# Two transformer blocks with a product-key expert layer on one core: gather rows of the first token tile brought forward, 76 instead of 64 expert columns spilled, their splits on VectorE

## The chip, the cores and the metric

The kernel runs on one core of one Trainium2 chip. The metric is the time of one execution on the device in microseconds (us). A comparison uses the median of several runs; the profile is of one execution.

The engines are named as in the profile: PE is TensorE (matmuls), DVE is VectorE, ACT is ScalarE, POOL is GpSimd, SP is the engine that issues most DMAs. Each takes its instructions in the order of the program.

## The reference

Two blocks, 512 tokens of width 1024, batch 1, all in float32. The first block mixes tokens by retention and by a sparse attention, then has a convolved feed-forward network (FFN). The second mixes by a gated linear recurrence and a short convolution; its last part is the expert layer that the change is about:

```python
q = (xb @ w_query).reshape(T, 8, 2, 128)                    # 8 heads, two halves
s = einsum('thpk,hpnk->thpn', q, sub_keys)                  # 128 scores per half
top_s, top_i = top_k(s, 16)
cand_s = top_s[:, :, 0, :, None] + top_s[:, :, 1, None, :]  # 16 x 16 pairs
best_s, best_pos = top_k(cand_s, 16); idx = ...             # of 128*128 = 16384 experts
gate = softmax(best_s)
act = gelu(einsum('td,thkd->thk', xb, expert_u[idx]))
out = einsum('thk,thkd->td', gate * act, expert_v[idx])
```

So each token has 8 x 16 = 128 experts, each with a row of `u` and a row of `v`. The result is scaled, added to `x`, and normalised.

## The kernel before

**Tiling.** The tokens lie in four tiles of 128. A float32 product on PE is made of three: each operand is split into a high and a low part of a rounded type (`split`, L195 to L202: the high part by ACT at L200, the low by DVE or POOL at L201), and `mm3` (L204 to L208) adds low x high, high x low and high x high. A pair of split buffers is taken from the pool `wsp` (8 pairs), what comes from DRAM lands in the pool `wraw` (3 buffers); `unit` (L189) does both for a piece of weights of 128 x 1024.

**The expert layer.** Tile 0 and tiles 1 to 3 are handled in two ways. For tile 0, each of the 128 experts of a token is fetched by an indirect DMA that POOL issues (`gather`, L1064): 128 rows of `u`, each followed by a dot product with the token on DVE (L1076), and 128 rows of `v`, each accumulated into `acc0` on DVE (L1078 or L1081). They use four buffers `grow`. For tiles 1 to 3, 384 tokens, all 16384 experts are computed densely: 128 columns of `u` with 128 experts each (`expert_in`, L1055), the activations times a dense gate matrix, and 128 columns of `v`.

**Stages.** `peer` (L1022) runs these stages one behind the other in the program:

1. `route`, first part: 16 query projections, each with its scores and `top16` on DVE.
2. `route`, second part: for each tile the top 16 of the 256 candidates and their indices and gates, nearly all on DVE (L1110 to L1154).
3. `gates_dense` (L1179): in 12 steps `c` of 32 tokens, each of eight groups `t4` of four tokens, two one-hot matrices `A` (`ga`) and `B` (`gb`) of 128 x 128 are built per token, and one matmul (L1215) makes the token's 128 x 128 gates. They go to DRAM (`gD`).
4. `experts_out` (L1225): for each of 128 columns `j`, activations times gates, split again, times the column of `v`.

Columns of `u` need only the tokens, so 64 of them (every even one) are computed early, between the steps of stages 1 to 3, and spilled to DRAM (`actD`); L1039 says after how many steps how many. In stage 4 they are read back; the odd ones are computed there. The gather begins with stage 4, and `GBY` spreads it over 120 columns.

**Who builds `A`.** `GP, GA = (2, 6), (0, 4)` at L35: groups 2 and 6 on POOL (L1198), 0 and 4 on ACT (L1202, L1203: |i - iota|, then relu(1 - that); the gate then goes into `B`, four narrow instructions at L1205), the others on DVE (L1209). `B` of the groups that are not ACT's is one wide compare on DVE (L1212).

**What sets the order.** The program is written in the order above, and a scheduler of the framework then orders the instructions of each engine: it runs its own model of time and, where an engine is free in it, takes the first instruction in the program that is ready. An instruction late in the program can so come early if all that it waits for is a buffer. Once built, the order is fixed, and engines wait for each other by semaphores.

## Time and profile before

| | |
|---|---|
| median of 3 runs | 2284.07 us (2283.7 to 2288.77) |
| profiled execution | 2284.71 us |
| its span | 2282.9 us |
| PE busy | 2202.7 us (96%) |
| DVE busy | 1655.5 us (73%) |
| ACT busy | 918.3 us (40%) |
| POOL busy | 793.9 us (35%) |
| moved by DMA | 469.53 MB, mean 206 GB/s |

The span runs from the first to the last instruction of the program. The shares are means over stages with different limits, so they say little about one stage: PE's 96% is of the whole span, and its busy time counts pipelined matmuls by modelled ends. The chain of waits on the page holds only the last instructions here, so the stages are read by windows, by lines, and by the order of single instructions. A line of the profile is that of the helper that records the instruction (L200, L201 and L206 to L208 are such), so the names of the tiles tell them apart.

### The profile page before, as it was taken

What the parts mean: (1) busy time and instruction counts of PE and PEld (TensorE: products, weight loads), DVE (VectorE), ACT (ScalarE), POOL (GpSimd) and SP (SyncE); (2) the same over time, 40 slices, a digit from 0 to 9 for tenths busy, and PEclk for the clock granted to TensorE, in tenths of its full rate; (3) what the DMA queues carried; (4) which work ended last, traced back from release to release, by engine and by line L of the source; (5) the groups of instructions that cost most, each with busy time, mean ns of one, the idle gap of its engine ahead of it and who ended that gap; (6) DMA issues with size and microseconds to landing.
All of it is one profiled execution on the core that took longest, in us unless ns stands there. A gap on an engine that the chain in (4) does not pass through costs nothing. (4 is left out here: it accounts for less than half of the span.)

```text
span 2282.9 us, 32142 instructions
## 1 busy us (share of the span) xinstructions
PE 2202.7 (96%) x11849; PEld 1956.0 (86%) x11849; DVE 1655.5 (73%) x3081; ACT 918.3 (40%) x1540; POOL 793.9 (35%) x603
## 2 busy tenths in 40 slices
PE   7998999999999999999998989989999999999998
PEld 6786888888889888889998989978888888888886
DVE  5347657788526478556589999678888787888878
ACT  4225444433325443343243467623333333333332
POOL 2223110000002233222366688634343434444445
PEclk9999999999999999999999999999999999999999
DMA  8323006766222221053345446799999999999996
GB/s 283 90 69 115 16 1 218 244 213 230 94 91 96 87 80 56 20 174 113 116 149 154 151 180 249 285 340 348 331 343 343 348 342 338 341 330 349 336 347 214
DMA packets 165645, 469.53 MB, mean 206 GB/s; under 512 B 18800, under 2 KB 62704, under 8 KB 165360
## 3 DMA queue, kind: packets, MB, share of 16 engines
q1 hardware_dynamic: 128624, 333.25, 42.4%
q0 software_dynamic: 36864, 134.23, 16.1%
q8 instruction: 93, 1.52, 0.3%
q14 instruction: 64, 0.52, 0.1%
HBM read 422.31 MB, written 39.85 MB: 202 GB/s over the span
## 5 line engine op out<-in xcount | busy, mean ns | idle before, releaser
L206 PE MATMUL b<-hh,wlo 128*128 128x384 f32 (+2 forms) x1872 | 658.0, 352 | 8.6 <-DVE wlo L201 3.1
L207 PE MATMUL b<-hl,whi 128*128 128x384 f32 (+2 forms) x1872 | 656.2, 351 | 3.4 <-DVE hl L288 3.3
L208 PE MATMUL b<-hh,whi 128*128 128x384 f32 (+2 forms) x1872 | 655.1, 351 | 0.0
L200 ACT ACTIVATE whi<-raw 128x1024 fp32r<-128x1024 f32 (+1 forms) x405 | 423.9, 1053 | 367.7 <-PE b L208 168.6
L201 DVE TENSOR_TENSOR wlo<-raw,whi 128x1024 fp32r<-128x1024 f32 x330 | 406.2, 1233 | 197.3 <-ACT whi L200 190.8
L206 PEld LDWEIGHTS b<-hh,wlo 128*128 128x128 f32 x1872 | 355.6, 190 | 37.1 <-issue 4.4
L207 PEld LDWEIGHTS b<-hl,whi 128*128 128x128 f32 x1872 | 356.1, 190 | 30.7 <-DVE hl L288 3.8
L201 POOL TENSOR_TENSOR wlo<-raw,whi 128x1024 fp32r<-128x1024 f32 x75 | 197.8, 2650 | 528.4 <-ACT whi L200 518.4
L208 PEld LDWEIGHTS b<-hh,whi 128*128 128x128 f32 x1872 | 356.5, 190 | 24.7
L206 PE MATMUL b<-whi,wl 128*128 128x512 f32 x768 | 299.6, 390 | 10.4 <-DVE wl L1261 10.4
L208 PE MATMUL b<-whi,wh 128*128 128x512 f32 x768 | 300.7, 392 | 0.0
L207 PE MATMUL b<-wlo,wh 128*128 128x512 f32 x768 | 300.6, 391 | 0.0
L1073 POOL DMA_INDIRECT grow<-in_p_ur_dram,eid x128 | 169.4, 1323 | 244.3 <-DVE gact L1076 163.7
L1073 POOL DMA_INDIRECT grow<-in_p_v_dram,eid x128 | 163.1, 1274 | 221.6 <-DVE acc L1078 137.9
L1061 ACT ACTIVATE act<-b 128x384 f32<-128x384 f32 x114 | 55.6, 490 | 345.4 <-PE b L208 300.0
L206 PE MATMUL b<-whi,hl 128*128 128x512 f32 (+1 forms) x464 | 178.9, 387 | 3.4 <-DVE hl L254 2.1
L206 PEld LDWEIGHTS b<-whi,wl 128*128 128x128 f32 x768 | 144.7, 188 | 39.4 <-DVE wl L1261 10.7
L208 PE MATMUL b<-whi,hh 128*128 128x512 f32 (+1 forms) x464 | 177.8, 384 | 0.0
L207 PE MATMUL b<-wlo,hh 128*128 128x512 f32 (+1 forms) x464 | 177.7, 383 | 0.0
L208 PEld LDWEIGHTS b<-whi,wh 128*128 128x128 f32 x768 | 144.5, 188 | 30.3
L207 PEld LDWEIGHTS b<-wlo,wh 128*128 128x128 f32 x768 | 144.7, 188 | 29.0
L1078 DVE SCALAR_TENSOR_TENSOR acc<-grow,gact,acc 128x1024 f32<-128x1024 f32 x127 | 163.1, 1284 | 3.2 <-DMA grow<-in_p_v_dram,eid 2.2
(296 smaller groups left out, 2979.1 us busy)
## 6 DMA issues: line engine op xcount, KB each, us to landing
raw<-in_p_u_dram SPq DMA_DIRECT2D x128, 512.0 KB, 4.4
raw<-in_p_v_dram SPq DMA_DIRECT2D x128, 512.0 KB, 6.5
raw<-in_w_adaT_dram SPq DMA_DIRECT2D x48, 512.0 KB, 4.1
gD<-gst SPq DMA_DIRECT2D x48, 512.0 KB, 4.4
gt<-gD SPq DMA_DIRECT2D x16, 1536.0 KB, 12.5
raw<-in_w_up_dram SPq DMA_DIRECT2D x44, 512.0 KB, 4.2
raw<-in_w_t_dram SPq DMA_DIRECT2D x32, 512.0 KB, 3.7
acts<-actD SPq DMA_DIRECT2D x64, 192.0 KB, 5.6
```

What stands on the lines that cost most here:

```text
L200: nc.scalar.activation(hi, raw, AF.Copy)
L201: (eng or nc.vector).tensor_tensor(lo, raw, hi.bitcast(F32), op=ALU.subtract)
L206: mm(out, al, bh, start=start, stop=False)
L207: mm(out, ah, bl, start=False, stop=False)
L208: mm(out, ah, bh, start=False, stop=stop)
L1061: self.nc.scalar.activation(act, ps, AF.Gelu)
L1073: nc.gpsimd.indirect_dma_start(out=g, out_offset=None, in_=rows[n], in_offset=bass.IndirectOffsetOnAxis(ap=self.eid[:, s:s + 1], axis=0))
L1078: nc.vector.scalar_tensor_tensor(self.acc0, g, act[:, s:s + 1], self.acc0, op0=ALU.mult, op1=ALU.add)
```

## The change

- `NSPILL` 64 becomes 76: 76 columns are spilled, spread over the 128, and 52 (`fresh`) are computed in stage 4. Spilled activations are 384 wide (`NIN`) as before.
- The pace (L1039 before) becomes five pieces of steps, columns, gather rows and the engine for the low part of the split: 1 step with 3 columns and 15 with 3 on POOL, then 8 with 10, 24 with 40 and 20 gather rows, 24 with 20 and 22 gather rows, the low part of all these on DVE. Before, all 64 were split on POOL. So 42 gather rows are written ahead of stage 4; their buffers `grow` now live in a pool opened ahead of stage 1.
- Gates: POOL builds `A` of three groups (1, 3, 6) instead of two. ACT puts the gate into `A` by four narrow instructions (relu(gate - gate x |i - iota|), with a fourth table of negated gates), and `B` is one wide compare on DVE in all eight groups. `ga` and `gb` have 4 buffers each instead of 6.
- Pools: `wsp` is closed and opened again ahead of the second mixer (8 pairs) and of the expert layer (6 pairs). In stage 4 two more raw buffers are used in turn with the three. Activations there lie in 8 buffers, and four instead of three columns are computed ahead.

```diff
-NSPILL = 64
+NSPILL = 76
+NIN = 384
-GP, GA = (2, 6), (0, 4)
+GP, GA = (1, 3, 6), (0, 4)
+NACT = 8
...
     def unit(self, src, eng=None):
-        raw = self.wraw.tile([128, 1024], F32, name="raw")[:, :src.shape[-1]]
+        self.turn = (self.turn + 1) % len(self.raws)
+        raw = self.raws[self.turn].tile([128, 1024], F32, name="raw")[:, :src.shape[-1]]
...
             if n == 2:
+                wsp.close()
                 late = ctx.enter_context(tc.tile_pool(name="late", bufs=1, reuse_waits="tile"))
                 self.h2 = late.tile([128, D], F32, name="h2")
+            if n > 1:
+                wsp.close()
+                wsp = ctx.enter_context(ExitStack())
+                self.wsp = wsp.enter_context(tc.tile_pool(name=f"wsp{n}", bufs=8 if n == 2 else 6, reuse_waits="tile"))
...
+            self.grows = c0.enter_context(tc.tile_pool(name="grows", bufs=GROWS, reuse_waits="tile"))
+            g0 = [self.gather(P)]
+            fresh = [j for j in range(128) if (j + 1) * (128 - NSPILL) // 128 > j * (128 - NSPILL) // 128]
...
-                pace = [(1, 3), (15, 10), (32, 37), (24, 14)]
+                pace = [(1, 3, 0, nc.gpsimd), (15, 3, 0, nc.gpsimd), (8, 10, 0, nc.vector), (24, 40, 20, nc.vector),
+                        (24, 20, 22, nc.vector)]
...
-                        for _ in range((i + 1) * us // steps - i * us // steps):
-                            act = self.expert_in(self.gpool or Q, psp, 2 * j, nc.gpsimd, "ga" if self.gpool else "act")
-                            nc.sync.dma_start(self.actD[j], act)
-                            j += 1
+                        for _ in range(part(cols)):
+                            act = (self.gpool or Q).tile([128, NIN], F32, name="act", bufs=4)
+                            j = todo.pop(0)
+                            self.expert_in(act, psp, j, eng)
+                            nc.sync.dma_start(self.actD[self.slot[j]], act)
+                        _advance(g0, part(r0))
...
-                    if t4 in GP:
-                        for i in range(4):
-                            nc.gpsimd.tensor_scalar(A[:, i], iota, ii[:, i:i + 1], gg[:, i:i + 1], op0=ALU.is_equal,
-                                                    op1=ALU.mult)
-                    elif t4 in GA:
+                    if t4 in GA:
+
                         for i in range(4):
                             nc.scalar.activation(A[:, i], iota, AF.Abs, bias=ii[:, i:i + 1], scale=-1.0)
-                        nc.scalar.activation(A, A, AF.Relu, bias=self.ones, scale=-1.0)
                         for i in range(4):
-                            nc.vector.tensor_scalar(B[:, i], iota, jj[:, i:i + 1], gg[:, i:i + 1], op0=ALU.is_equal,
-                                                    op1=ALU.mult)
+                            nc.scalar.activation(A[:, i], A[:, i], AF.Relu, bias=gg[:, i:i + 1], scale=ng[:, i:i + 1])
                     else:
+                        eng = nc.gpsimd if t4 in GP else nc.vector
                         for i in range(4):
-                            nc.vector.tensor_scalar(A[:, i], iota, ii[:, i:i + 1], gg[:, i:i + 1], op0=ALU.is_equal,
-                                                    op1=ALU.mult)
-                    if t4 not in GA:
-                        nc.vector.tensor_tensor(B, iota[:, None, :].to_broadcast([128, 4, 128]),
-                                                jj[:, :, None].to_broadcast([128, 4, 128]), op=ALU.is_equal)
+                            eng.tensor_scalar(A[:, i], iota, ii[:, i:i + 1], gg[:, i:i + 1], op0=ALU.is_equal,
+                                              op1=ALU.mult)
+                    nc.vector.tensor_tensor(B, iota[:, None, :].to_broadcast([128, 4, 128]),
+                                            jj[:, :, None].to_broadcast([128, 4, 128]), op=ALU.is_equal)
...
+            more = c0.enter_context(tc.tile_pool(name="wraw2", bufs=2, reuse_waits="tile"))
+            self.raws = self.raws * 3 + [more] * 2
...
+            acts = [P.tile([128, n], F32, name=f"acts{i}") for i in range(NACT)]
+            free = list(range(NACT))
+            early = {}
+            for j in fresh[:4]:
+                early[j] = acts[free.pop(0)]
+                self.expert_in(early[j], psp.only("pre"), j, nc.vector)
```

The order that the scheduler makes of it differs in three places that matter below. The first is POOL in the gate stage. Before, POOL's compares for the gates (`ga`) stand between the splits of spilled columns (`wlo`), and the last 64 of them stand alone, ahead of all row issues (`grow`):

```order
166 L201 TENSOR_TENSOR wlo<-raw,whi 128x1024
167 L1198 TENSOR_SCALAR ga<-c_iota,sel_8238,sel_8240 128x128 x8
168 L201 TENSOR_TENSOR wlo<-raw,whi 128x1024
169 L1198 TENSOR_SCALAR ga<-c_iota,sel_8238,sel_8240 128x128 x4
170 L201 TENSOR_TENSOR wlo<-raw,whi 128x1024
171 L1198 TENSOR_SCALAR ga<-c_iota,sel_8238,sel_8240 128x128 x64
172 L1073 DMA grow<-in_p_ur_dram,eid 128x1024 x16
```

After, POOL has no splits there; row issues stand between its compares:

```order
196 L1080 DMA grow<-in_p_v_dram,eid 128x1024 x2
197 L1223 TENSOR_SCALAR ga<-c_iota,sel_8249,sel_8251 128x128 x4
198 L1080 DMA grow<-in_p_v_dram,eid 128x1024 x2
199 L1223 TENSOR_SCALAR ga<-c_iota,sel_8249,sel_8251 128x128 x8
200 L1080 DMA grow<-in_p_v_dram,eid 128x1024 x2
201 L1223 TENSOR_SCALAR ga<-c_iota,sel_8249,sel_8251 128x128 x4
202 L1080 DMA grow<-in_p_v_dram,eid 128x1024
```

In the whole order 53 row issues stand ahead of the first of 144 compares and 48 more between the first and the last.

The second is DVE in the gate stage. Before, narrow compares (`ga` at L1209, `gb` at L1205) and wide ones (`gb` at L1212):

```order
1294 L1209 TENSOR_SCALAR ga<-c_iota,sel_8238,sel_8240 128x128 x4
1295 L1212 TENSOR_TENSOR gb<-c_iota,sel_8239 128x512
1296 L1205 TENSOR_SCALAR gb<-c_iota,sel_8239,sel_8240 128x128 x4
1297 L1212 TENSOR_TENSOR gb<-c_iota,sel_8239 128x512
1298 L1209 TENSOR_SCALAR ga<-c_iota,sel_8238,sel_8240 128x128 x4
1299 L1212 TENSOR_TENSOR gb<-c_iota,sel_8239 128x512 x2
```

After, more wide compares, splits of `u` (`wlo`) and the accumulation or dot product of gathered rows (`acc`, `grow`) among fewer narrow ones:

```order
1405 L204 TENSOR_TENSOR wlo<-raw,whi 128x1024
1406 L1225 TENSOR_TENSOR gb<-c_iota,sel_8250 128x512
1407 L1095 SCALAR_TENSOR_TENSOR acc_8240<-grow,gact,acc_8240 128x1024
1408 L1223 TENSOR_SCALAR ga<-c_iota,sel_8249,sel_8251 128x128 x4
1409 L1225 TENSOR_TENSOR gb<-c_iota,sel_8250 128x512 x2
1410 L1095 SCALAR_TENSOR_TENSOR acc_8240<-grow,gact,acc_8240 128x1024
1411 L1225 TENSOR_TENSOR gb<-c_iota,sel_8250 128x512
1412 L204 TENSOR_TENSOR wlo<-raw,whi 128x1024
```

Between the first and the last gate instruction of DVE there are 144 narrow and 96 wide compares, 13 splits and 48 rows.

The third is DVE while tiles are routed. Before, only the routing itself (`eq`, `si`, `g`, `best`, `pos`):

```order
1219 L1127 CAST abf<-ab 128x256
1220 L1135 TENSOR_TENSOR eq<-abf,c_iota 128x1024 x2
1221 L1147 TENSOR_REDUCE gs<-g 128x8
1222 L1137 TENSOR_TENSOR eq<-eq,fi 128x2048
1223 L1148 RECIPROCAL gs<-gs 128x8
1224 L1140 TENSOR_REDUCE si_11151<-eq 128x128
```

After, with splits and rows in it:

```order
1288 L1166 TENSOR_TENSOR g<-g,gs 128x128
1289 L204 TENSOR_TENSOR wlo<-raw,whi 128x1024
1290 L1095 SCALAR_TENSOR_TENSOR acc_8240<-grow,gact,acc_8240 128x1024
1291 L1152 TENSOR_TENSOR eq<-eq,fi 128x2048
1292 L1195 MAX_INDEX pos<-best,rest 128x8
1293 L204 TENSOR_TENSOR wlo<-raw,whi 128x1024
```

From the last score's top 16 to the first gate instruction 47 splits and 50 rows stand among the routing. On PE, 6.8 columns of `u` lie among the query projections (14.7 before), 50 in the routing, 18.2 between the first and the last gate matmul, 2 behind it (3.3 before), and 48 in stage 4 (60 before). On ACT, the first splits of the second mixer's weights stand behind the last squares of the FFN's last tile, where two of them stood ahead of those of the first tile.

## Rows read from the trace of the kernel before

**Rows 1.** Windows: stretch, us, busy us per engine (instructions), clock, DMA share, GB/s

```profile
996.00:1156.00 160.00, 160.00 (x851) 145.06 (x851) 86.73 (x490) 52.45 (x76) 46.36 (x20) 1.00 0.34 115
1156.00:1320.00 164.00, 146.69 (x819) 145.16 (x817) 163.47 (x367) 65.17 (x96) 106.15 (x39) 0.96 0.50 153
1320.00:1465.00 145.00, 144.35 (x1104) 144.28 (x1105) 138.15 (x360) 110.12 (x236) 122.73 (x99) 0.99 0.62 232
1465.00:1494.00 29.00, 15.86 (x79) 15.15 (x78) 11.17 (x17) 8.99 (x15) 4.42 (x5) 0.83 0.99 361
1494.00:2272.00 778.00, 777.63 (x3744) 684.43 (x3742) 639.28 (x827) 269.29 (x380) 331.83 (x255) 1.00 0.92 333
```

**Rows 2.** Timeline of PE: start us, us, engine, line, operation, shape, count

```profile
1194.69 0.33 PE L206 MATMUL b<-hh,wlo 128*128 128x384 f32 x1
...
1198.85 0.33 PE L206 MATMUL b<-hh,wlo 128*128 128x384 f32 x1
...
1346.58 2.84 PE L1215 MATMUL b<-gb,ga 128*128 128x128 f32 x24
1349.18 0.42 PE L207 MATMUL b<-hl,whi 128*128 128x384 f32 x1
```

**Rows 3.** Lines, 1156 to 1320 us: count, busy us, mean ns, idle before

```profile
L1135 DVE TENSOR_TENSOR eq<-abf,c_iota 128x1024 f32<-128x1024 f32 x16 | 32.1, 2047 | 0.0
L1137 DVE TENSOR_TENSOR eq<-eq,fi 128x2048 f32<-128x2048 f32 x8 | 21.8, 2730 | 0.0
L1140 DVE TENSOR_REDUCE si<-eq 128x128 f32<-128x2048 f32 x8 | 18.2, 2280 | 0.0
L1110 DVE TENSOR_TENSOR cand<-val 128x2048 f32<-128x2048 f32 x4 | 11.7, 2915 | 0.0
L1205 DVE TENSOR_SCALAR gb<-c_iota,sel,sel 128x128 f32<-128x128 f32 x4 | 5.2, 1355 | 0.0
...
L201 POOL TENSOR_TENSOR wlo<-raw,whi 128x1024 fp32r<-128x1024 f32 x35 | 101.5, 2917 | 56.2 <-ACT whi L200 52.7 <-PE b L206 3.5
```

**Rows 4.** Line 1135 by itself: shortest, median, longest ns

```profile
L1135 DVE TENSOR_TENSOR eq<-abf,c_iota x16: 1214/1257/3425, 1190.4 to 1305.7; 128x1024 f32<-128x1024 f32 x16
```

**Rows 5.** Lines of DVE and POOL, 1320 to 1465 us

```profile
L1209 DVE TENSOR_SCALAR ga<-c_iota,sel,sel 128x128 f32<-128x128 f32 x188 | 61.0, 404 | 2.5 <-DMA actD<-ga 2.0 <-PE b L1215 0.5
L1212 DVE TENSOR_TENSOR gb<-c_iota,sel 128x512 f32<-128x512 f32 x72 | 48.2, 688 | 0.0
L201 DVE TENSOR_TENSOR wlo<-raw,whi 128x1024 fp32r<-128x1024 f32 x8 | 9.8, 1229 | 0.0
...
L1198 POOL TENSOR_SCALAR ga<-c_iota,sel,sel 128x128 f32<-128x128 f32 x92 | 109.3, 1198 | 20.6 <-PE b L1215 12.2 <-ACT gst L1217 3.7 <-issue 1.8
```

**Rows 6.** Timeline of DVE, 1388 to 1392 us

```profile
1388.49 1.31 DVE L201 TENSOR_TENSOR wlo<-raw,whi 128x1024 fp32r<-128x1024 f32 x1
1389.73 1.10 DVE L1209 TENSOR_SCALAR ga<-c_iota,sel,sel 128x128 f32<-128x128 f32 x4
1390.74 0.69 DVE L1212 TENSOR_TENSOR gb<-c_iota,sel 128x512 f32<-128x512 f32 x1
1391.35 0.85 DVE L1209 TENSOR_SCALAR ga<-c_iota,sel,sel 128x128 f32<-128x128 f32 x3
```

**Rows 7.** Line 1198 by itself

```profile
L1198 POOL TENSOR_SCALAR ga<-c_iota,sel,sel x96: 782/1079/3122, 1308.0 to 1460.1; 128x128 f32<-128x128 f32 x96
```

**Rows 8.** Timeline of POOL and DVE, 1645 to 1650 us

```profile
1647.48 1.86 POOL L1073 DMA_INDIRECT grow<-in_p_v_dram,eid  x1 [1.79 <-DVE acc L1078]
1649.65 0.93 POOL L1073 DMA_INDIRECT grow<-in_p_v_dram,eid  x1 [0.30 <-issue]
...
1645.93 2.60 DVE L1078 SCALAR_TENSOR_TENSOR acc<-grow,gact,acc 128x1024 f32<-128x1024 f32 x2
1648.44 1.22 DVE L201 TENSOR_TENSOR wlo<-raw,whi 128x1024 fp32r<-128x1024 f32 x1
```

**Rows 9.** Lines of DVE, 1495 to 2272 us

```profile
L1076 DVE CUSTOM_DVE_ANT_0 grow<-grow,h 128x1024 f32<-128x1024 f32 x126 | 152.5, 1222 | 1.5 <-DMA grow<-in_p_ur_dram,eid 1.5
```

More of the change, by code (lines that the diff above doesn't have):

```diff
@@ L1033, in peer @@
             self.gate0 = P.tile([128, 128], F32, name="gate0")
+            self.grows = c0.enter_context(tc.tile_pool(name="grows", bufs=GROWS, reuse_waits="tile"))
+            g0 = [self.gather(P)]
+            fresh = [j for j in range(128) if (j + 1) * (128 - NSPILL) // 128 > j * (128 - NSPILL) // 128]
+            self.slot = {j: k for k, j in enumerate(j for j in range(128) if j not in fresh)}
             with ExitStack() as c1:
@@ L1055, in expert_in @@
-    def expert_in(self, pool, psp, j, eng, tag="act"):
-        n = S - 128
+            self.experts_out(fresh, g0, sum(p[2] for p in pace))
+    def expert_in(self, act, psp, j, eng):
         w = self.unit(self.a["p_u"][j], eng=eng)
-        ps = psp.tile([128, S], F32, name="u")[:, :n]
-        self.proj_t(ps, w, self.hh, self.hl, slice(128, S))
-        act = pool.tile([128, S], F32, name=tag, bufs=6)[:, :n] if tag == "ga" else pool.tile([128, n], F32, name=tag, bufs=4)
+        ps = psp.tile([128, S], F32, name="u")[:, :NIN]
+        self.proj_t(ps, w, self.hh, self.hl, slice(S - NIN, S))
@@ L1061, in expert_in, with row @@
         self.nc.scalar.activation(act, ps, AF.Gelu)
-        return act
+    def row(self, n, eid):
+        g = self.grows.tile([128, D], F32, name="grow")
+        self.nc.gpsimd.indirect_dma_start(out=g, out_offset=None, in_=self.a[n].rearrange("j i d -> (j i) d"),
+                                          in_offset=bass.IndirectOffsetOnAxis(ap=eid, axis=0))
+        return g
     def gather(self, P):
-        tc, nc, a = self.tc, self.nc, self.a
-        rows = {n: a[n].rearrange("j i d -> (j i) d") for n in ("p_ur", "p_v")}
+        nc = self.nc
@@ L1071, in gather @@
                 for s in range(16 * h, 16 * h + 16):
-                    g = P.tile([128, D], F32, name="grow", bufs=GROWS)
-                    nc.gpsimd.indirect_dma_start(out=g, out_offset=None, in_=rows[n],
-                                                 in_offset=bass.IndirectOffsetOnAxis(ap=self.eid[:, s:s + 1], axis=0))
+                    g = self.row(n, self.eid[:, s:s + 1])
                     if n == "p_ur":
@@ L1232, in experts_out @@
             P = c0.enter_context(tc.tile_pool(name="eo", bufs=1, reuse_waits="tile"))
-            gather = [self.gather(P)]
-            _advance(gather)
             T = c0.enter_context(tc.tile_pool(name="eow", bufs=2, reuse_waits="tile"))
+            more = c0.enter_context(tc.tile_pool(name="wraw2", bufs=2, reuse_waits="tile"))
+            self.raws = self.raws * 3 + [more] * 2
             psp = _Banks(self.psum, u=[4, 5], pre=[0, 1, 2], acc=[0, 1, 2, 3, 6, 7])
             g2 = self.gate_row(P, psp.only("u"), 40, "g2")
-            early = {j: self.expert_in(T, psp.only("pre"), j, nc.vector) for j in (1, 3, 5)}
+            acts = [P.tile([128, n], F32, name=f"acts{i}") for i in range(NACT)]
[4 more added lines that the diff above has]
+                self.expert_in(early[j], psp.only("pre"), j, nc.vector)
             acc = [[psp.tile([128, 512], F32, name="acc") for h in range(2)] for t in range(NT - 1)]
@@ L1247, in parts @@
                                       self.gD[:, :, 256 * g:256 * g + 256].rearrange("c i n -> i c n"))
-                if j % 2 == 0:
-                    act = T.tile([128, n], F32, name="acts", bufs=3)
-                    nc.sync.dma_start(act, self.actD[j // 2])
-                elif j in early:
-                    act = early.pop(j)
-                else:
-                    act = self.expert_in(T, psp, j, nc.vector)
+                if j in early:
+                    act = early[j]
+                else:
+                    act = acts[free[0]]
+                    if j in self.slot:
+                        nc.sync.dma_start(act, self.actD[self.slot[j]])
+                    else:
+                        self.expert_in(act, psp, j, nc.vector)
+                    free.append(free.pop(0))
+                if j in early:
+                    free.append(acts.index(early.pop(j)))
                 v = self.unit(a["p_v"][j])
```

45 lines of the change are left out of this document (23 added, 22 removed).

## Prediction, made before the changed kernel ran

> **What bounds the kernel now.** I read the stretches first, then the lines of the two vector engines in two of them, then single instructions. The windows [rows 1] cut the last mixer's work into five stages. From 996 us the query projections run: PE is busy all the 160 us, DVE 87. From 1156 us the four token tiles are routed: DVE is busy 163.5 of 164 us and PE waits 17, so DVE sets the pace. From 1320 us the dense gates are built: PE 144 of 145, DVE 138, POOL 123, three engines close together. From 1465 us PE waits half of 29 us for the gates to go to DRAM and come back. From 1494 us experts are multiplied out, and PE is busy 777.6 of 778 us with DVE at 639 and DMA at 0.92: PE sets the pace there.
>
> All that the change moves is in these five stages. PE's work in sum stays the same: a column of activations that is spilled early is not computed late. One column is 24 matmuls; from 1194.69 to 1198.85 us they take 4.16 us [rows 2]. So the question is how much longer PE stands still ahead of 1494 us. Now that is 498 us less the busy 160 + 147 + 144 + 16, or 31 us.
>
> **The change part by part, by the order of the changed program.**
>
> Query projections: 7.9 columns fewer lie between the first query matmul and the last score matmul (6.8 for 14.7). PE bounds the stage, so 7.9 x 4.16 = 33 us go: 160 becomes 127. DVE takes over splits, but has 73 us free there.
>
> Routing. PE gets 50 columns, 50 x 4.16 = 208 us. DVE gets its own work without POOL's splits beside it, plus two new kinds. Own work: a 1024-wide comparison (L1135) takes 2.05 us in the mean and 1.21 at best [rows 3, 4], because POOL's splits of 2.9 us hold it up; 16 x 0.84 = 13 us go. The 2048-wide passes L1137 and L1110 take 2.73 and 2.92 where the reduction of that width takes 2.28: 8 x 0.45 + 4 x 0.64 = 6 us go. The first gate group (5 us) now comes later. So 163 becomes 139. New: 47 splits of u at 1.24 us from start to next start [rows 6] are 58 us; and gather rows. The diff asks for 20 rows here, but the order puts 50 on DVE before its first gate instruction, because the scheduler brings forward what only waits for a buffer: 34 dot products at 1.22 [rows 9] and 16 accumulations at 1.25 (two in 2.51 us [rows 8]) are 62 us. The sum is 259; neighbours overlap by some 0.08 us (0.69 long, next start after 0.61 [rows 6]), so I take 250. Ends: 208, if PE were the bound, and 259. That is 86 us more than 164, and PE waits about 40 of it. POOL issues only rows here, and the landing is covered by four buffers.
>
> Gates. PE: 768 passes at 2.60/24 = 0.108 us [rows 2] are 83 us, and 18.2 columns 76, in sum 159. DVE: 144 compares at 1.01/4 us, 96 wide compares at 0.61, 13 splits at 1.24 [rows 6] and 48 more rows at 1.24 are 36 + 59 + 16 + 60 = 170. It was 138 with twice the narrow compares. ACT, busy 110 of 145 us [rows 1], gets 96 narrow activations for 24 wide ones; at DVE's 0.40 us for a narrow compare [rows 5] that is under 39 more, hidden below 170. The term that decides is POOL. It builds three groups of four in every eight, 144 compares where it built 96, and the order puts 48 row issues between them (53 rows ahead of its first compare, 101 by its last). One compare takes 0.78 us at best [rows 7], a row issue 0.93 [rows 8]: 113 + 45 = 158 us with nothing in the way.
>
> But something is in the way. The row issue at 1647.48 us took 1.86 us, and the DVE accumulation beside it ended 1.05 us after the issue began; the next, at 1649.65, took 0.93 [rows 8]. In the gate stage POOL's compare takes 1.20 us in the mean and 3.12 at most [rows 5, 7]. I read this as POOL standing still while DVE runs an instruction with two SBUF tensors. DVE had 48.2 + 9.8 = 58 us of those in the stage [rows 5], and POOL lost 92 x (1.198 - 0.782) = 38 us, 66% of it. The change removes POOL's own splits, but gives DVE 59 + 16 + 60 = 135 us of two-input work there: all wide compares, splits, dot products, accumulations. 66% of that is 89, so POOL needs 158 + 89 = 247 us. Ends: 170, where nothing holds POOL and DVE decides, and 158 + 135 = 293. I take 247, as the row nearest is of the same instruction in the same stage. So the stage grows from 145 to 247 us, and PE waits 88 us of it. POOL's compare is waited for by the gate matmul, PE takes its instructions in order, and with four gate buffers instead of six no engine can run far ahead.
>
> The Trainium skill, "GPSIMD Engine Reference", section "1. Specifications", says the same of two-input instructions, and also that DVE instructions in a two-port mode contend with GpSimd. By that second half the narrow compares, if they run in that mode, would hold POOL too, 66% of 36 us, and the time would be 24 us longer; no row here shows that mode.
>
> Gates to experts: the same chain (last copy, store, load, multiply, split). Two columns cover it instead of 3.3, more raw buffers may win a little back; I leave 29 us, with 24 to 36 as ends.
>
> Experts out: 12 columns fewer, 50 us, so 778 becomes 728. PE is bound with 0.4 us free, so fewer rows, an eased DMA, five raw buffers and eight activation buffers gain nothing beyond that. Six split pairs could cost; DVE's 139 us of slack [rows 1] and pairs that live for three columns make that 0, with 28 us as the far end (the 29 us stage's worth of starving once).
>
> Second mixer's start: its first splits now lie in new buffers over the old ones and stand on ACT behind the FFN's last sums. ACT's half and a DVE split of 1.23 us [rows 5] stand between the last FFN matmul and the next product: 2 to 8 us, I take 4.
>
> Sum: -33 + 86 + 102 + 0 - 50 + 4 = +109 us. The profiled execution took 2284.71 us (span 2282.9), the median of three is 2284.07; they agree. 2284.7 + 109 gives 2394; I forecast 2390 us, 4.6% slower. Its own range, with gates between 205 and 293 and routing between 240 and 259, is 2345 to 2440.
>
> **Rivals.**
>
> POOL is not held much (20%). If DVE leaves POOL alone, as its wide compares come in pairs and POOL could work in between, DVE's 170 us decide the gates: 2390 - 77 = 2313 us. For it: POOL idled 20.6 us in the stage before. Against it: 66% of two-input time was lost there.
>
> PE stays the bound (7%): faster. Place: routing and gates. If DVE's routing sum came under PE's 208 us and POOL built its group of four with its rows in 159/36 = 4.4 us, the 18 us that PE waits before 1465 us would go: 2284.7 - 18 + 4 = 2271. For it: PE was 99% busy in the gates, and DVE is rid of 24 us of holds and of half its narrow compares. Against it: a group is four compares and 1.3 row issues, 4 x 0.78 + 1.3 x 0.93 = 4.3 us at their shortest, so the smallest hold breaks it.
>
> No change (5%): the moves cancel, 2278 to 2291. Nothing makes them cancel; it would take 108 us of error.
>
> PE falls to its lower clock in the gates (8%). In the stretch from 1465 us, where PE waited most, the granted clock was 0.83 in the mean, in the bound stages 1.00 [rows 1]. If the short waits kept it at 1.2 instead of 2.4 GHz, its 159 us would be 318 and pass POOL's 247: 2390 + 71 = 2461.
>
> That the change doesn't do what its words say holds in part already: 101 rows, not 42, are issued before the last gate. With 42 rows, 20 fewer two-input instructions would lie in the gates; I count the order, as it is what runs.
>
> **How the numbers follow.** Forecast 60%, POOL not held 20%, lower clock 8%, PE bound 7%, no change 5%. What a measurement of this kernel can tell from no change is about 0.3%. Faster has only the PE case, 0.07; same 0.05; slower the rest, 0.88. The range of 2300 to 2440 leaves out the first two (12%) and the lower clock (8%).
>
> **What the changed profile would show.** Right: between the first and last gate matmul some 250 us, POOL's compares at about 1.4 us in the mean or more, PE busy near 65% there and waiting for POOL's `ga`; routing with DVE full for some 250 us; experts out near 728 us at full PE. Wrong: POOL's compare staying at 1.2 us or less with PE over 90% in the gates; routing under 220 us; or waits of PE in the last stage, which would be the six pairs.

## The result, and the profile after

The changed kernel takes 2421.47 us in the median of five runs (2415.65 to 2423.43), the kernel before 2285.49 (2283.7 to 2292.72): a ratio of 1.0587, 95% interval 1.0569 to 1.0605. The forecast was 2390 us, with a range of 2300 to 2440. The profiled executions have spans of 2420.7 and 2282.9 us, 137.8 us apart; the sum of the prediction gave 109.

The windows of the changed kernel, cut at the same events as [rows 1] (columns: stretch, its us, busy us and count of PE, PE's weight loads, DVE, ACT, POOL, granted clock, DMA share, GB/s):

```profile
996.00:1137.00 141.00, 133.36 (x683) 114.91 (x682) 95.60 (x500) 45.88 (x67) 7.17 (x3) 1.00 0.32 105
1137.00:1398.00 261.00, 211.91 (x1205) 210.85 (x1204) 251.99 (x501) 90.57 (x133) 87.42 (x58) 0.90 0.74 248
1398.00:1653.00 255.00, 205.25 (x1224) 190.48 (x1223) 179.45 (x316) 135.11 (x313) 242.72 (x189) 0.87 0.67 230
1653.00:1687.00 34.00, 10.91 (x48) 10.74 (x48) 16.55 (x27) 9.58 (x15) 11.06 (x10) 0.60 0.98 359
1687.00:2413.00 726.00, 725.67 (x3457) 633.23 (x3456) 520.65 (x662) 258.11 (x364) 204.75 (x155) 1.00 0.79 283
```

In [rows 1] PE was full or nearly so in three of the five stretches, and waited 17 us in the routing. Now it is full in the last alone. In the routing (second row) DVE is busy 252 of 261 us, in the gates (third) POOL 243 of 255. The same cut at events (first and last score matmul, first and last gate matmul, first and last product of the last stage), in us; the forecasts were made for the windows of [rows 1], which differ by up to 6 us from these:

| stage | before | after | difference | forecast |
|---|---|---|---|---|
| work ahead of the first score | 1001.4 | 1003.8 | +2.4 | +4 |
| query projections | 154.3 | 132.7 | -21.6 | -33 |
| routing | 165.0 | 261.9 | +96.9 | +86 |
| gates | 144.1 | 254.5 | +110.4 | +102 |
| gates to experts | 28.7 | 34.1 | +5.4 | 0 |
| experts out | 778.2 | 725.6 | -52.6 | -50 |
| behind the last product | 11.3 | 8.0 | -3.3 | 0 |

What PE waited for in the query projections, the routing and the gates, one row each (waiting instruction, the one waited for, us in total, times, longest):

```profile
PE b L1119 <- ACT q L1116: 5.6, 8, 0.7
...
PE b L1182 <- DVE si L1157: 48.7, 3, 38.6
...
PE b L1228 <- POOL ga L1223: 48.8, 47, 5.3
```

In the routing PE ran out of columns and stood ahead of a transpose until DVE had the tile's indices. In the gates it waited 47 times for a group that POOL built. The lines of POOL and DVE in the gates, 1398 to 1653 us, answer to [rows 5]:

```profile
L1223 POOL TENSOR_SCALAR ga<-c_iota,sel,sel 128x128 f32<-128x128 f32 x140 | 182.3, 1308 | 1.5 <-PE b L1228 0.4
L1080 POOL DMA_INDIRECT grow<-in_p_v_dram,eid x27 | 33.7, 1247 | 6.1 <-issue 5.5 <-ACT ga L1217 0.3 <-PE b L1228 0.3
L1080 POOL DMA_INDIRECT grow<-in_p_ur_dram,eid x22 | 29.2, 1326 | 4.6 <-issue 4.1 <-DVE ga L1223 0.5
...
L1225 DVE TENSOR_TENSOR gb<-c_iota,sel 128x512 f32<-128x512 f32 x92 | 63.1, 699 | 10.8 <-PE b L1228 9.1 <-PE b L209 1.5
L1223 DVE TENSOR_SCALAR ga<-c_iota,sel,sel 128x128 f32<-128x128 f32 x140 | 46.8, 426 | 40.2 <-PE b L1228 38.2 <-PE b L209 1.9
L1095 DVE SCALAR_TENSOR_TENSOR acc<-grow,gact,acc 128x1024 f32<-128x1024 f32 x29 | 37.9, 1307 | 12.3 <-DMA grow<-in_p_v_dram,eid 12.2
L1093 DVE CUSTOM_DVE_ANT_0 grow<-grow,h 128x1024 f32<-128x1024 f32 x21 | 26.0, 1247 | 9.4 <-DMA grow<-in_p_ur_dram,eid 9.4
L204 DVE TENSOR_TENSOR wlo<-raw,whi 128x1024 fp32r<-128x1024 f32 x13 | 16.0, 1230 | 2.9 <-ACT whi L203 2.9
```

POOL's compare takes 1.31 us in the mean where 0.78 is the least. Ahead of its compares it idles 1.5 us in all, while DVE waits 40 us for PE: PE follows POOL, and DVE follows PE. One stretch of the timeline shows what a compare loses its time to (start, us, engine, line):

```profile
1499.87 3.12 POOL L1223 TENSOR_SCALAR ga<-c_iota,sel,sel 128x128 f32<-128x128 f32 x4
...
1508.72 2.83 POOL L1223 TENSOR_SCALAR ga<-c_iota,sel,sel 128x128 f32<-128x128 f32 x1
...
1501.38 1.69 DVE L1223 TENSOR_SCALAR ga<-c_iota,sel,sel 128x128 f32<-128x128 f32 x4 [3.72 <-PE b L1228]
...
1508.63 0.68 DVE L1225 TENSOR_TENSOR gb<-c_iota,sel 128x512 f32<-128x512 f32 x1
1509.23 1.22 DVE L204 TENSOR_TENSOR wlo<-raw,whi 128x1024 fp32r<-128x1024 f32 x1
1510.37 0.68 DVE L1225 TENSOR_TENSOR gb<-c_iota,sel 128x512 f32<-128x512 f32 x1
```

Four compares from 1499.87 us took 3.12 us, 0.78 each, with DVE's one-input compares beside the last two. One compare from 1508.72 took 2.83: 2.05 more than its 0.78, while DVE ran wide compares and a split without a pause. Fitted over all 144 compares (length against the time that each kind of DVE instruction lies beside it), a compare takes 0.69 us, plus 0.62 us for each us of wide compares, 0.86 for each us of splits and row work, and 0.1 for each us of narrow compares; this explains 94% of the variance.

### The profile page after: what moved, and what is told of

Read it like the earlier page. It is cut to its first block, busy times and chain, and to the rows that moved or that the text cites. A ratio compares the mean times of both kernels' runs of the same rounds, so it can differ in the third digit from the quotient of the medians.

```text
span 2420.7 us, 32156 instructions
## 1 busy us (share of the span) xinstructions
PE 2242.3 (93%) x11849; PEld 1980.3 (82%) x11849; DVE 1674.2 (69%) x3019; ACT 944.0 (39%) x1615; POOL 727.4 (30%) x593
## 5 line engine op out<-in xcount | busy, mean ns | idle before, releaser
L204 DVE TENSOR_TENSOR wlo<-raw,whi 128x1024 fp32r<-128x1024 f32 (+1 forms) x388 | 476.5, 1232 | 258.3 <-ACT whi L203 241.2
L1080 POOL DMA_INDIRECT grow<-in_p_v_dram,eid x128 | 177.0, 1383 | 240.6 <-DVE acc L1095 155.1
L236 POOL TENSOR_SCALAR ss<-ss 128x1 f32<-128x1 f32 x28 | 11.5, 410 | 657.4 <-ACT junk L232 439.7
L1223 POOL TENSOR_SCALAR ga<-c_iota,sel,sel 128x128 f32<-128x128 f32 x144 | 188.0, 1311 | 1.6 <-PE b L1228 0.4
L1228 PE MATMUL b<-gb,ga 128*128 128x128 f32 x768 | 134.9, 314 | 49.7 <-POOL ga L1223 48.8
L1093 DVE CUSTOM_DVE_ANT_0 grow<-grow,h 128x1024 f32<-128x1024 f32 x128 | 155.2, 1223 | 28.5 <-DMA grow<-in_p_ur_dram,eid 28.5
L1228 PEld LDWEIGHTS b<-gb,ga 128*128 128x128 f32 x768 | 119.3, 218 | 64.3 <-POOL ga L1223 62.8
```

The source lines that it names most:

```text
L204: (eng or nc.vector).tensor_tensor(lo, raw, hi.bitcast(F32), op=ALU.subtract)
L236: nc.gpsimd.tensor_scalar(ss[:, 3:4], ss[:, 0:1], ss[:, 1:2], eps, op0=ALU.add, op1=ALU.add)
L1080: self.nc.gpsimd.indirect_dma_start(out=g, out_offset=None, in_=self.a[n].rearrange("j i d -> (j i) d"), in_offset=bass.IndirectOffsetOnAx ...
L1093: nc.vector.tensor_tensor_reduce(g, g, self.h2, 1.0, 0.0, ALU.mult, ALU.add, act[:, s:s + 1])
L1223: eng.tensor_scalar(A[:, i], iota, ii[:, i:i + 1], gg[:, i:i + 1], op0=ALU.is_equal, op1=ALU.mult)
L1228: nc.tensor.matmul(ps.rearrange("p (j t) -> p t j", t=4)[:, i, :], A[:, i, :], B[:, i, :], start=True, stop=True)
```

## The experiments

The theory after the result has two parts: POOL bounds the gates, held by DVE's two-input work, and DVE bounds the routing by splits and rows. Each part had rivals: in the gates PE's lower clock, or the third group alone; in the routing the landing of the rows. The stages by the same events, the time behind the last product (tail) and the medians, in us; the last column is the 95% interval of the ratio to the kernel before, which was measured again beside each set of runs:

| kernel | routing | gates | experts | tail | median | ratio, interval |
|---|---|---|---|---|---|---|
| before | 165.0 | 144.1 | 778.2 | 11.3 | 2285.49 | |
| changed | 261.9 | 254.5 | 725.6 | 8.0 | 2421.47 | 1.0569 to 1.0605 |
| two groups on POOL | 261.5 | 206.2 | 725.5 | 8.1 | 2377.54 | 1.0377 to 1.0426 |
| rows late | 193.4 | 183.1 | 727.9 | 61.9 | 2337.00 | 1.0201 to 1.0252 |
| one-input rows | 281.4 | 210.6 | 727.1 | 8.1 | 2402.05 | one run |
| before, three groups | 160.1 | 167.7 | 777.7 | 18.5 | 2313.32 | 1.0087 to 1.0137 |
| splits of u on POOL in the routing | 245.9 | 266.2 | 727.2 | 8.1 | 2423.12 | 1.0568 to 1.0610 |
| 40 rows early, splits on POOL | 245.5 | 187.9 | 727.0 | 8.6 | 2334.44 | 1.0191 to 1.0230 |
| the same, 4 columns moved | 217.4 | 193.1 | 728.6 | 9.5 | 2329.55 | 1.0168 to 1.0205 |
| 28 rows early, splits on DVE | 206.3 | 179.5 | 727.4 | 29.4 | 2317.38 | 1.0100 to 1.0142 |
| 70 columns, 18 rows early | 197.6 | 166.8 | 752.2 | 24.9 | 2318.73 | 1.0124 to 1.0167 |
| rows late, six buffers | 193.4 | 182.5 | 727.5 | 50.2 | 2327.66 | 1.0174 to 1.0206 |
| 64 columns, splits on POOL | 180.5 | 154.2 | 777.5 | 20.8 | 2317.96 | 1.0137 to 1.0168 |
| 64 columns, splits on DVE | 190.4 | 149.9 | 778.0 | 16.1 | 2321.21 | 1.0148 to 1.0177 |

**Two groups on POOL.**

```
-GP, GA = (1, 3, 6), (0, 4)
+GP, GA = (2, 6), (0, 4)
```

> The changed kernel with two gate groups of eight on GpSimd instead of three (DVE takes the third; rows, splits and everything else stay). Theory (GpSimd bounds the gates: its compares and row issues, plus what DVE's two-input work holds it): 96 compares at 0.78 us are 75, some 47 row issues at 0.93 are 44, the hold of about 90 us stays, so 209 us where 144 compares took 254; DVE, with 48 more narrow compares, needs some 200, close behind. Gates 205 to 220 us, the whole 2375 to 2390. Rival (PE bounds the gates at its lower clock, granted 0.87 there, and the wait for GpSimd only fills its gaps): gates stay at 245 us or more, the whole 2410 or more.

Measured: gates 206.2 us, the whole 2377.54. The expectation of 205 to 220 holds, and the rival of PE's clock, 245 or more, falls. 48 compares fewer on POOL gave 48 us, although DVE got them.

**Rows that read one tensor.**

```
-tensor_tensor_reduce(g, g, self.h2, ..., act[:, s:s + 1])
+tensor_reduce(act[:, s:s + 1], g, AX.X, ALU.add)
-scalar_tensor_tensor(self.acc0, g, act[:, s:s + 1], self.acc0, ...)
+tensor_reduce(self.acc0[:, s:s + 1], g, AX.X, ALU.add)
```

> The changed kernel in which DVE's work on each gathered row reads one tensor of 1024 instead of two (a plain sum of the row in place of the dot product with h2 and in place of the weighted accumulation), so the gathered part of tile 0 is not computed; issues, transfers, compares, splits stay. Theory (GpSimd stands still while DVE runs an instruction with two SBUF inputs): in the gates GpSimd loses some 45 us less, its compare falls from 1.31 us in the mean to near 1.05, and the stage from 254 to some 210 us. Rival (it is the busy DVE, or the row transfers, whatever the number of inputs): compare stays at 1.25 us or more and the stage at 245 us or more. The routing may grow by some 20 us, since 75 rows instead of 53 come ahead of the gates, so the stage is to be read and not the whole.

Gates 210.6 us, POOL's lines there:

```profile
L1222 POOL TENSOR_SCALAR ga<-c_iota,sel,sel 128x128 f32<-128x128 f32 x138 | 144.2, 1052 | 1.1
L1080 POOL DMA_INDIRECT grow<-in_p_v_dram,eid x30 | 32.0, 1066 | 6.8 <-issue 4.7 <-DVE gb L1224 0.9 <-DVE ga L1222 0.5
L1080 POOL DMA_INDIRECT grow<-in_p_ur_dram,eid x21 | 23.2, 1103 | 4.9 <-issue 3.5 <-DVE ga L1222 0.6 <-DVE gb L1224 0.3
```

The compare fell from 1.31 us to 1.05, the issue of a v row from 1.25 to 1.07 and of a u row from 1.33 to 1.10, with 51 row issues in the stage where there were 49. DVE was nearly as long busy with a row (1.21 us, 1.25 to 1.31 in the changed kernel), and the DMA share was higher (0.81 for 0.67). So neither a busy DVE nor the transfers hold POOL. The new instructions also write one number where the old ones wrote 1024; that this isn't the reason is seen at the narrow compares, which write a whole tensor and read one: in the fit they cost POOL next to nothing. What is left is the second tensor that DVE reads. Here the theory was tested most directly, and both its numbers came out. This is a single run, of which only the stage is read.

**Rows late.** The row buffers and the first row are in the last stage again, and the pace asks for no rows (0 for the 20 and 22):

```
 # peer
-self.grows = c0.enter_context(tc.tile_pool(name="grows", bufs=GROWS, ...))
-g0 = [self.gather(P)]
+g0 = []
 # experts_out
+self.grows = c0.enter_context(tc.tile_pool(name="grows", bufs=GROWS, ...))
+gather = [self.gather(P)]
+_advance(gather)
```

> The changed kernel with the gather's buffers and its first row only in the last stage, as before the change, so that no row is issued, multiplied or summed while tiles are routed and gates built; three groups on GpSimd stay. Theory (rows cost DVE's time in the routing and GpSimd's twice in the gates, by the issue and by the hold): routing falls from 262 us to PE's own 200, gates to 113 for compares plus 0.62 of 63 us of wide compares plus 0.86 of 28 us of splits, some 176, with PE's 173 beside it. The whole is 2283 to 2303; the upper end if the last stage, with all 257 rows in 12 columns less time, is held by DMA. Rival (the third group on GpSimd is the cost, rows little): gates stay near 230 us and the whole near 2350.

Windows of the gates, the last stage and the time behind the last product:

```profile
1328.00:1511.00 183.00, 180.88 (x1308) 180.09 (x1307) 123.56 (x255) 143.21 (x326) 156.24 (x136) 0.99 0.58 216
...
1543.00:2270.50 727.50, 727.50 (x3456) 634.55 (x3455) 596.90 (x777) 251.32 (x349) 299.68 (x230) 1.00 0.93 334
2270.50:2332.00 61.50, 0.03 (x1) 0.00 (x0) 41.04 (x51) 5.33 (x17) 32.94 (x33) 0.53 0.66 226
```

Routing and gates are PE's again, 193 and 183 us, as the theory said: without rows they are 68 and 71 us shorter, though the third group is still on POOL. (The new order also moved 3.6 columns from the routing to the gates.) But the whole was 34 us over my range's upper end. The last product ended at 2270.5 us, 1 us earlier than in the kernel before; then DVE still had 24 rows to work on (16 accumulations, 8 dot products; the 34 that later expectations name counted other instructions with them). So early rows also save: the last stage, shorter by 12 columns, can't take all 256 rows (257 in the expectation is a miscount).

**The kernel before with three groups on POOL.**

```
-GP, GA = (2, 6), (0, 4)
+GP, GA = (1, 3, 6), (0, 4)
```

> The kernel before with only its gate groups on GpSimd changed, from two of eight to three (DVE's fall from four narrow groups to three); no row is gathered there and splits of u stay on GpSimd. Theory: GpSimd needs 144 compares at 0.78, 113 us, plus the 38 us that DVE's two-input work held it before, plus 13 us of splits, 164 us for the 145 before: the whole 2295 to 2312. Rival (GpSimd's compare is slow only beside the rows and splits that the change put on DVE, and PE stays the bound): gates within 3 us of 145, the whole within 0.3% of before.

```profile
1321.00:1489.00 168.00, 156.71 (x1113) 152.64 (x1114) 131.84 (x315) 109.61 (x236) 166.41 (x147) 0.96 0.55 204
```

POOL is full, the gates take 167.7 us for the 164 expected, and the whole, 2313.32, is 1.3 us over the range (the tail grew by 7). The third group costs 24 us by itself in the kernel before; in the changed kernel, with 49 rows and DVE's two-input work beside it, 48.

**Splits of u on POOL again in the routing.**

```
-(8, 10, 0, nc.vector), (24, 40, 20, nc.vector),
+(8, 10, 0, nc.gpsimd), (24, 40, 20, nc.gpsimd),
```

> The changed kernel with the splits of u in the routing on GpSimd again; rows, three groups and the gates' own splits on DVE stay. Theory (in the routing DVE sets the end, by its own work, the splits and the rows, and a split on GpSimd costs it some 0.65 us of hold where its own cost 1.24): DVE's 252 us lose 58 and gain some 30 of holds on its other work, PE has 46 columns, 192 us, so the routing takes 200 to 225 us where it took 262; the gates, with four columns more beside a full GpSimd, 254 to 262. The whole 2365 to 2390. Rival (the landing of the rows sets the routing's end, or GpSimd, which now has splits of 2.9 us and rows in one queue): routing 245 us or more, the whole 2405 or more.

The theory's numbers fell here: the routing took 245.9 us for 200 to 225, and the whole is no faster than the changed kernel. DVE's lines of this kernel in the routing, and one of POOL:

```profile
L1093 DVE CUSTOM_DVE_ANT_0 grow<-grow,h 128x1024 f32<-128x1024 f32 x25 | 45.0, 1813 | 0.0
L1095 DVE SCALAR_TENSOR_TENSOR acc<-grow,gact,acc 128x1024 f32<-128x1024 f32 x15 | 35.6, 2376 | 0.0
L1150 DVE TENSOR_TENSOR eq<-abf,c_iota 128x1024 f32<-128x1024 f32 x16 | 32.1, 2045 | 0.0
...
L204 POOL TENSOR_TENSOR wlo<-raw,whi 128x1024 fp32r<-128x1024 f32 x42 | 108.2, 2583 | 16.5 <-ACT whi L203 16.0
```

and the same three of the changed kernel, with the splits on DVE:

```profile
L1093 DVE CUSTOM_DVE_ANT_0 grow<-grow,h 128x1024 f32<-128x1024 f32 x32 | 38.7, 1214 | 4.7 <-DMA grow<-in_p_ur_dram,eid 4.7
L1095 DVE SCALAR_TENSOR_TENSOR acc<-grow,gact,acc 128x1024 f32<-128x1024 f32 x18 | 23.1, 1282 | 0.0
L1150 DVE TENSOR_TENSOR eq<-abf,c_iota 128x1024 f32<-128x1024 f32 x16 | 18.9, 1222 | 0.0
```

It wasn't the rival's landings or POOL's queue either: DVE is busy 245 of 246 us. Its dot products grew from 1.2 to 1.8 us, its comparisons to 2.05, its accumulations from 1.3 to 2.4. In the timeline of this kernel:

```profile
1220.87 2.40 POOL L204 TENSOR_TENSOR wlo<-raw,whi 128x1024 fp32r<-128x1024 f32 x1
...
1220.74 3.62 DVE L1093 CUSTOM_DVE_ANT_0 grow<-grow,h 128x1024 f32<-128x1024 f32 x1
```

The dot product takes its own 1.22 us and the whole 2.40 of POOL's split. Without the 60.8 us of splits that the changed kernel has on DVE, and ten rows of 1.24, DVE's 252 us would be 179; it was busy 245, so 42 splits on POOL cost it 66 us, 1.6 each and not 0.65. My 0.65 came from a routing in which DVE ran fewer two-input instructions; rows are two-input work.

**40 rows early, two groups, splits on POOL; and the same with four columns in the projections instead of the routing.** Drawn from the version with rows late:

```
-GP, GA = (1, 3, 6), (0, 4)
+GP, GA = (2, 6), (0, 4)
-g0 = []
+g0 = [self.gather(P)]                    # and none ahead of experts_out
-(8, 10, 0, nc.vector), (24, 40, 0, nc.vector), (24, 20, 0, nc.vector)]
+(8, 10, 0, nc.gpsimd), (24, 40, 24, nc.gpsimd), (24, 20, 16, nc.vector)]
+self.grows = self.gpool or self.rpool    # the gates' pool, or the routing's
 # the second: (15, 7, ...) for (15, 3, ...), (24, 36, ...) for (24, 40, ...)
```

> A version drawn from the runs so far: the changed kernel with two groups on GpSimd, the splits of u in the routing on GpSimd, and 40 rows ahead of the last stage: 24 from buffers that live only while tiles are routed, 16 from buffers that live only while gates are built, so that no more can come forward. Theory: routing is PE's 46 columns, 192 us and the transposes, some 198 (DVE 149 of work and 30 of holds); gates PE's 174 (GpSimd 66 for compares, 44 and 38 for holds, 19 for rows, 167); the last stage 728 with its rows done before its last product (34 were left where all 257 were to be done in it). 1002 + 133 + 198 + 176 + 31 + 728 + 10 is 2278 by the profile's span, 2275 to 2290 as median: 0.2 to 0.4% under before. Rival (each row ahead of the gates costs DVE or GpSimd its full time on the path): 2320 or more.

> The version with 40 early rows, with four columns moved from the routing to the query projections, so that more columns stand between a query's product and its scores. Theory (PE waited 5.6 us there for ACT's copy of q, which a column covers): the projections take 133 + 3 x 4.16 less some 4, about 141 us; routing loses four columns, 16 us, if DVE's 152 us and its holds stay under PE's 182. In sum 3 to 6 us under the version with four columns fewer there. Rival (DVE sets the routing's end as soon as columns leave it): no gain, or a loss of up to 10 us.

The first missed its range by 44 us, as its routing took 245.5 us for 198. DVE was busy 240 us of that: beside POOL's splits its comparisons took 2.05 us and its dot products 2.14, and the order had put 32 of the 40 rows there, not 24. Its gates, 188 for 176, and its tail, 8.6, came nearer. The second gained 4.9 us, within the 3 to 6 expected, and the projections took 141.8 us for 141. But the terms differ: the routing fell by 28 us, not 16, with eight rows fewer in it, while the work ahead of the scores and the gates grew by 6 and 5.

**Splits on DVE, 28 or 18 rows early, 76 or 70 columns.**

```
-(15, 7, 0, nc.gpsimd), (8, 10, 0, nc.gpsimd), (24, 36, 24, nc.gpsimd), (24, 20, 16, nc.vector)]
+(15, 7, 0, nc.gpsimd), (8, 10, 0, nc.vector), (24, 38, 6, nc.vector), (24, 18, 22, nc.vector)]
 # 70 columns: NSPILL = 70, (24, 34, 4, ...), (24, 16, 14, ...)
```

> The changed kernel with the splits of u on DVE as the change has them, two groups on GpSimd, 28 rows ahead of the last stage (6 from buffers that live while tiles are routed, 22 from buffers that live while gates are built), and four columns moved from the routing to the query projections. Theory (a two-input instruction of one of the two engines stops one of the other: splits on GpSimd stretched DVE's rows and comparisons in the two versions before this, splits on DVE don't, as GpSimd only issues a few rows in the routing): DVE's routing sum is 178 by its rows without holds, some 190 with landings, under PE's 48 columns, 201; gates 155 to 168 (GpSimd 66 for compares, 41 and 30 of holds, 26 for rows; PE 148). 1003 + 141 + 201 + 163 + 28 + 727 + 9 is 2272: 2265 to 2285. Rival (any 28 early rows lengthen the stages by as much as they save): 2295 or more.

> The same with 70 columns spilled in place of 76 and 18 rows early (4 and 14), so that DVE and GpSimd have less to do in the routing and the gates and the last stage six columns more. Theory: routing is PE's 44 columns, 184 us (DVE 172 to 180), gates PE's 141 with DVE and GpSimd at some 145 each, 147; the last stage 727 + 25. 1003 + 141 + 184 + 147 + 28 + 752 + 9 is 2264: 2258 to 2280, under the version with 76 columns. Rival (the gates still wait for GpSimd, and the six columns come on top): 2285 or more.

The routing took 206 and 198 us for 201 and 184. With the splits off POOL, DVE's comparisons and dot products take 1.22 us or less again in both, which bears out the reading of the run on splits. How much of the shorter routing comes from that, and how much from its 8 and 5 early rows where the version before had 24, these runs don't separate. Both wholes missed: the gates took 179.5 and 166.8 us for 163 and 147 (PE waited for POOL's compares again, some 12 us in each), and the tail, where the last rows are worked on, 29 and 25 for 9.

**Six row buffers, rows late.**

```
-GROWS = 4
+GROWS = 6
```

> The version with all rows in the last stage, with six row buffers instead of four. There 34 rows were left after the last product, a tail of 62 us; a row took 3.2 us in the mean, as in the kernel before, with the DMA engines 0.93 busy. If the DMA engines set that rate, six buffers change nothing: the tail stays at 50 us or more, the whole within 5 us of 2337. If it is the time from a buffer's release to the next row's landing, 3.2 us go toward 2.8 (PE's 727 us over 257 rows), the tail shrinks to 15 us or less and the whole comes to 2285 to 2295.

```profile
1543.00:2270.00 727.00, 725.80 (x3450) 633.84 (x3451) 599.08 (x783) 252.76 (x350) 301.82 (x233) 1.00 0.93 337
```

The tail is 50 us for 62, and the DMA engines stay at 0.93, as with four. The whole gained 9 us: a little more than the first case allowed, and far from the second, with a tail of 15. So buffers aren't the main limit of the rows. That the DMA engines are it is likely from their share, and not shown.

**64 columns, rows late, two groups,** splits of u in the routing on POOL, then on DVE:

```
-NSPILL = 76
+NSPILL = 64
-GP, GA = (1, 3, 6), (0, 4)
+GP, GA = (2, 6), (0, 4)
-(15, 3, 0, nc.gpsimd), (8, 10, 0, nc.vector), (24, 40, 0, nc.vector), (24, 20, 0, nc.vector)]
+(15, 10, 0, nc.gpsimd), (8, 10, 0, nc.gpsimd), (24, 32, 0, nc.gpsimd), (24, 9, 0, nc.vector)]
 # the second: (8, 10, 0, nc.vector), (24, 30, 0, nc.vector), (24, 11, 0, nc.vector)]
```

> Rows late, two groups on GpSimd and 64 columns as in the kernel before, its splits of u in projections and routing on GpSimd as there; what stays of the change is the gate form (the gate in ACT's last pass, one wide comparison for every group), six pairs, five raw buffers, eight activation buffers, and 39 columns in the routing where there were 34, 9 to 11 in the gates where there were 13. Theory (the change's loss is the rows and the third group; the rest is small): routing 168 (DVE's 139 and 0.65 of hold for each of 39 splits, PE 163), gates 138 (PE 45 for columns and 90 for passes), last stage 774, tail 11: the whole 2268 to 2283. Rival (one of the parts that stay costs too): 2295 or more.

> The same with the splits of u in the routing on DVE, as the change has them, and 41 columns there. Theory (without rows, GpSimd's splits hold DVE 0.65 us each and DVE's own cost 1.16): routing 184 us, DVE's 139 and 44, gates 130, the whole 5 to 15 us over the version with splits on GpSimd. Rival (a split costs DVE the same on either engine, as it stands still for it): within 3 us of that version.

In the first the theory fell: 2317.96 us, 35 over the range's upper end. Early rows, the third group and the 12 further columns are gone, and it is still 34 us slower than the kernel before, so some of the parts that stay cost too. The routing took 180.5 us for 168 (0.65 us of hold for a split was too small here too), the gates 154.2 for 138, the tail 20.8 for 11. What waited in its gates (us in total, times, longest):

```profile
PE b L1227 <- POOL ga L1222: 12.8, 25, 0.8
...
DVE ga L1222 <- PE b L1227: 11.4, 23, 1.7
DVE gb L1224 <- PE b L1227: 11.1, 19, 2.1
...
POOL ga L1222 <- PE b L1227: 52.3, 21, 16.7
```

No engine is full (PE is busy 140.5 of 154 us), and POOL and DVE wait for PE while PE waits for POOL. The change cut the gate buffers from six to four. That four are too few would fit these rows, but six beside the new gate form weren't tried, so this cause stays open, and so does that of the longer tail. The second is 3.2 us slower, with overlapping ranges, and lies between its theory (5 to 15) and its rival (within 3). Which engine splits cheaper without rows stays open.

No version is faster than the kernel before. Nearest of those drawn from the change came the one with 28 early rows, at 1.012.

## Why the prediction was right, point by point

The direction, the engine that bounds each stage and the place of nearly all the loss came out. The whole took 31 us more than forecast: queries, routing and gates came out 8 to 11 us over their terms each, and the step from gates to experts 5. By the steps:

- **Query projections.** The 7.9 columns were counted from the first query matmul; between the first and the last score lie 13.8 columns before and 6.8 now, so 29 of the 33 us belong to this stage. PE's busy time there fell by 27, from 154.3 us to 127.1. Left out were 5.6 us that PE waits for ACT's copy of q: before, a column stood between each of the 16 products and its scores, now between 9 of them. With four more columns ahead of the routing all 16 are covered again, and PE's waits for that copy fall to 2.9 us.
- **Routing.** DVE was to be busy 250 us and was, 252; PE was to wait about 40, and waited 48.7. Missing are DVE's own waits of 10 us: rows landing 4.7, which I had called covered, high halves from ACT 3.9, and scores 1.4. That the holds by POOL's splits would go is shown: the comparison fell from 2.05 us [rows 3] to 1.22, the reduction stayed at 2.28.
- **Gates.** The forecast of 247 us was 158 bare and 89 of hold. POOL lost 182.3 - 140 x 0.782 = 73 us in compares and 62.9 - 49 x 0.93 = 17 in issues, 90 in all, of DVE's 143 us of two-input work: 63%, where 66% of 135 was forecast. That 89 and 90 agree so well is partly luck, as both factors were off. 10.7 us of gaps ahead of the issues make the rest. The reading of [rows 8] was too strict: the issue at 1647.48 us ended while DVE's split, which also reads two tensors, was still running, so POOL doesn't stand still for all of DVE's two-input work; the share of 66% allowed for that. PE's own term was low: 768 passes take about 90 us, as 144.35 [rows 1] less the 13.1 columns of 4.16 that lie there says, not the 83 of one undisturbed row [rows 2]. At the clock of 0.87 they took longer still, so PE was busy 80% of the stage, not near 65%, and waited 48.8 us, not 88. POOL hid this error.
- **Rivals.** That POOL is not held is out, by the one-input rows. PE's clock did fall, to 0.87, and its passes grew from 0.278 to 0.314 us; but PE still waited 48.8 us, POOL idled only 1.5 us ahead of its compares, and with two groups the stage was 48 us shorter at a clock of 0.95. So the lower clock was an effect, not the bound. PE as the bound is out too: in the routing it was busy 212 us, DVE 252.
- **Gates to experts.** 34 us for 29, inside the ends given: PE had 10.9 us of work to cover the stores where it had 15.9 before.
- **Experts out.** 725.6 us at full PE for 728: no wait of PE shows for the six pairs, the raw or the activation buffers. What I had wrong is the value of early rows, "fewer rows gain nothing": with all 256 rows late the tail is 62 us. The 101 early rows paid for part of what they cost, and the prediction, which counted the order as it is, was right here without knowing it.
- **Order.** The 42 early rows that the change asks for became 101. The scheduler brings a row forward as soon as a buffer is free, so the lifetime of the buffers decides, not the table of the pace: with buffers that live in one stage only, just the 18, 28 or 40 rows asked for came early.
- **The range.** By the terms given with it, gates 205 to 293 and routing 240 to 259, the prediction's own range adds up to 2338 to 2445, not 2345 to 2440. The measured time lies inside both.

The prediction weighed the Trainium skill, "GPSIMD Engine Reference", section "1. Specifications". Its half on two SBUF inputs agrees with the fit (0.86 us a us). For its half on two-port modes no run shows which mode the narrow compares use. Beside them POOL's compare isn't held, so the 24 us that the prediction weighed for this didn't come: 45 compares with under 0.04 us of two-input work beside them took 0.78 to 0.83 us, with narrow compares beside them for 0 to 1.03 us.

## What to carry to other kernels

When work moves from GpSimd to DVE or back, price what it stops on the other engine, not only its own time: count the tensors that each instruction reads, and don't let both engines run two-input work in the same stage unless neither paces it. Where a GpSimd instruction paces PE, add to its shortest time most of the two-input time that DVE runs meanwhile (63% of it here). Work brought forward must go where an engine idles, and what it relieves later (here the row work of the last stage) is worth counting too.

## What the runs showed of the hardware

The hold goes both ways. When a split on GpSimd meets two-input instructions of DVE, either of them can be the one that waits for all of the other. In the run with splits on POOL it was DVE's dot product: 1.22 us became 3.62 beside a split of 2.40. In the kernel before there are splits that waited instead:

```profile
1190.37 4.65 POOL L201 TENSOR_TENSOR wlo<-raw,whi 128x1024 fp32r<-128x1024 f32 x1
...
1190.40 2.35 DVE L1135 TENSOR_TENSOR eq<-abf,c_iota 128x1024 f32<-128x1024 f32 x2
```

The two comparisons took their usual 1.22 us each, and the split its own 2.40 and most of their 2.35. The recorded starts don't tell which one waits: the dot product is recorded 0.13 us ahead of its split, this split 0.03 us ahead of the comparisons. A split also stops DVE's narrow compare, which reads one tensor, and its cast. In the kernel before:

```profile
1313.74 2.33 POOL L201 TENSOR_TENSOR wlo<-raw,whi 128x1024 fp32r<-128x1024 f32 x1
...
1313.78 2.38 DVE L1205 TENSOR_SCALAR gb<-c_iota,sel,sel 128x128 f32<-128x128 f32 x1
```

The compare, 0.34 us otherwise, ended with the split. The cast of idx took 1.39 us in the mean in the run with splits on POOL and 0.29 in the changed kernel. DVE's reductions, maxima and index searches didn't slow in that run (2.27 us for 2.28 in the changed kernel, 0.41 for 0.42). GpSimd's own narrow compare stops no DVE instruction that the rows show (in the changed kernel wide compares take 0.70 us beside it and 0.69 without, narrow ones 0.41 and 0.38), yet it is slowed by DVE's two-input ones. The Trainium skill, "SBUF — State Buffer", section "SBUF: two separate sides", calls the shared pair of ports an exclusive lock, held for a whole instruction; the 3.62 and 4.65 us agree, while 0.62 us a us for wide compares, whose two inputs are repeated along an axis, is less than a full stop.
